# Stick-breaking attention: the cumulative sum as two float32r parts, the scores over 64 rows a head, and the gates of the two mixers summed by products with ones

## The chip, the cores and the metric

One core of a Trainium2 chip runs the whole program in one launch. The metric is device microseconds of that core; the time before the change is the median of three runs.

## What is computed

Two residual layers over 256 tokens of width 1024, float32 throughout. Layer 0 mixes tokens by stick-breaking attention, layer 1 by retention; each is followed by a mixture of 16 experts. A vector `c` modulates every sub-layer by shift, scale and gate (`adaLN`), and every sub-layer ends in a layer norm.

```python
def adaln_params(c, w, b):
    m = jax.nn.silu(c) @ w + b
    shift, scale, gate = jnp.split(m, 3, axis=-1)
...
# stick_breaking_attention, 16 heads of 64, one block of 128 queries
z = jnp.einsum('bhqd,bhkd->bhqk', qb, k) * scale
causal = key_pos[None, :] < q_pos[:, None]
log_keep = jnp.where(causal, jax.nn.log_sigmoid(-z), 0.0)
suffix = lax.cumsum(log_keep, axis=3, reverse=True) - log_keep
a = jnp.where(causal, jnp.exp(jax.nn.log_sigmoid(z) + suffix), 0.0)
o = jnp.einsum('bhqk,bhkd->bhqd', a, v)
...
x = layer_norm(DEEPNORM_ALPHA * x + (1.0 + gate) * y, ln_g[i, 0], ln_b[i, 0])
```

The gate of a mixer is thus a row of 1024 numbers, `1 + silu(c) @ w + b`, that multiplies the output of the mixer's last projection on every token.

## The kernel before

**Stages.** The program passes through attention (`STICK`), the first mixture (`SPARSE`), retention (`RETEN`) and the second mixture. Weights stream from memory through a ring of 1 MB buffers; SP issues all their transfers in one queue, and a transfer waits there until its buffer is free. A scheduler sets the order of the instructions on every engine when the program is built: it takes the order in which the code emits them as priority and its own estimate of durations, so each engine's queue is fixed when the program runs.

**Dense products.** `dense_feat` (L431) and `dense_tok` (L405) multiply by weights in two float32r parts. `pieces` (L384) loads 512 rows of weights and splits them in two pieces of 128x1024 numbers: ACT copies the piece to float32r (L381), DVE subtracts the copy from it (L382). Both parts lie in one buffer of the tag `w2`, which in the attention stage means one of the two `wp` buffers. `mm3` (L400) then makes three products a block (L401 to L403).

**Modulation.** `ada_part(i, j)` (L266) computes 512 columns of `silu(c) @ w` of sub-layer `i`; `j` 0 and 1 are the shift, 2 and 3 the scale, 4 and 5 the gate. Either TensorE makes the products (L277), or DVE does, by eight passes over 128x512 (L280, L282), which leave partial sums in every partition. Four products with two columns of ones (L292, `rest`) sum over the partitions and turn the result into columns, and DVE adds the bias (L293, L296). `plan` lists such parts and `fill` emits the next one between two dense products; the `rest` of a part is emitted at the following `fill`. Before a mixer's last projection `gate_row` (L351) turns the gate's columns into a row that stands in all partitions: eight products (L235) and two ACT copies (L357). Sub-layers 0 and 2 are the two mixers, 1 and 3 the mixtures.

**Attention.** It goes in two halves of eight heads. `stick_in` (L572) makes queries, keys and values of a half. Queries go to `qz`, where each head's 64 rows stand alone in 128 rows of zeros (L575, L579, L580), so that a product over 128 rows gives one head's scores. `stick_attn` (L590) takes two heads at a time, four times a half:

```python
a = z + causal                              # L600, DVE
e = ln(1 + exp(-|a|))                       # L602 to L604, ACT
e = max(a, 0) + e                           # L605, DVE: -log_keep
sx = negtri @ e, mones @ e[later keys]      # L608, L609, TensorE, float32
a = exp(a + sx)                             # L610 DVE, L611 ACT
o = v @ a                                   # L615, L616, TensorE
oh, ol = split_to(o)                        # L381 ACT, L382 DVE
```

Here L597 and L598 make the scores `z`. After the two halves `out_proj` (L558) multiplies by `sb_w_out` column half by column half; L564 multiplies by the gate, L565 adds to the residual. The router (`logits`) and the first mixture follow.

**Places in memory.** `HIGH` gives every name a place in the numbered slots. The two halves' `qz` fill slots 2 and 3; the mixture's first weights want slots 2, 4, 0 and 1 (`RINGS["moe1"]`).

## Time and profile before

| what | value |
|---|---|
| median of 3 runs | 924.22 us (921.85 to 925.86) |
| the profiled execution, its time / its span | 924.58 us / 922.9 us |
| TensorE busy | 852.6 us, 92% of the span |
| DVE busy | 500.6 us, 54% |
| ACT busy | 275.7 us, 30% |
| memory read | 307.12 MB, 334 GB/s over the span |

The span is what the profiler saw between first and last instruction; the execution took 1.7 us more. A busy share is a mean over stages with different limits, so it has to be read stage by stage. A matmul in a row of matmuls begins long before the one ahead of it has ended: the time that one costs is read from start to start, not from its duration. DVE's instructions overlap by some 0.09 us in the same way.

### The profile page before, as it was taken

The page shows a single profiled execution, that of the slowest core. Times are in us where ns is not written, and L with a number is a line of the kernel's source. Part 1 is how long each engine was busy: PE and PEld are TensorE (multiplying, and loading weights), DVE is VectorE, ACT ScalarE, POOL GpSimd, SP SyncE. Part 2 cuts the span into 40 slices and gives each one's busy share as a digit, 9 for nine tenths or more (in the row PEclk, how much of TensorE's full clock was granted, in tenths as well). Part 3 has the DMA queues.
Part 4 walks back from the last instruction along what each step waited for, and adds up shares of the span by engine and source line. Part 5 has one row for each costly group of instructions (what it writes and reads, how often), then busy time and mean ns, then how long its engine had stood idle before and what let it go on. Part 6 is the DMA issues. An engine that isn't in the chain of part 4 may idle for free. (4 is left out here: it accounts for less than half of the span.)

```text
span 922.9 us, 11147 instructions
## 1 busy us (share of the span) xinstructions
PE 852.6 (92%) x4339; PEld 522.0 (57%) x4339; DVE 500.6 (54%) x927; ACT 275.7 (30%) x386; POOL 25.5 (3%) x46
## 2 busy tenths in 40 slices
PE   5899999989969999999799999999979989999994
PEld 2598887765324434334578888888843444343331
DVE  1478889835341326321797898948655322333126
ACT  1446756252110101000544455646351101011010
POOL 1000000000000000000000020011000000000000
PEclk9999999979999999999899999999979999999998
DMA  8999998796999999999669778939739999999951
GB/s 304 384 387 387 335 330 310 288 368 228 420 413 386 417 420 414 417 406 357 224 227 363 275 274 273 320 101 361 299 134 390 415 416 418 415 415 418 416 221 45
DMA packets 93075, 309.01 MB, mean 335 GB/s; under 512 B 5876, under 2 KB 6316, under 8 KB 77140
## 3 DMA queue, kind: packets, MB, share of 16 engines
q1 hardware_dynamic: 93012, 308.19, 86.9%
q8 instruction: 37, 0.61, 0.3%
q14 instruction: 26, 0.21, 0.1%
HBM read 307.12 MB, written 1.05 MB: 334 GB/s over the span
## 5 line engine op out<-in xcount | busy, mean ns | idle before, releaser
L964 PE MATMUL ps<-s,xg 128*64 128x512 f32 x632 | 164.8, 595 | 1.4 <-DVEq L842 1.4
L964 PE MATMUL ps<-w,xg 128*64 128x512 f32 x392 | 113.2, 606 | 6.5 <-PEq L842 6.5
L964 PEld LDWEIGHTS ps<-s,xg 128*64 128x64 f32 x632 | 50.7, 137 | 85.7 <-issue 81.8
L382 DVE TENSOR_TENSOR wp<-w,wp 128x1024 fp32r<-128x1024 f32 x57 | 69.5, 1222 | 20.3 <-ACT wp L381 19.1
L381 ACT ACTIVATE wp<-w 128x1024 fp32r<-128x1024 f32 x57 | 59.8, 1056 | 66.2 <-PE ps L403 55.6
L1044 PE MATMUL ps<-w,hidT 128*64 128x512 f32 x248 | 71.4, 596 | 7.2 <-DVE hidT L1007 6.6
L997 DVE TENSOR_TENSOR mosg<-mosg,ps 128x512 f32<-128x512 f32 x16 | 11.0, 688 | 122.0 <-PE ps L964 122.0
L381 ACT ACTIVATE moyh<-moy 128x512 fp32r<-128x512 f32 x32 | 20.1, 629 | 174.0 <-DVE moy L1017 174.0
L489 DVE TENSOR_TENSOR res<-res,ps 128x512 f32<-128x512 f32 x64 | 41.0, 684 | 57.0 <-PE ps L1029 57.0
L964 PEld LDWEIGHTS ps<-w,xg 128*64 128x64 f32 x392 | 34.8, 139 | 64.6 <-issue 62.7
L282 DVE SCALAR_TENSOR_TENSOR s<-w,cact,s 128x512 f32<-128x512 f32 x88 | 65.9, 749 | 0.7
L1017 DVE SCALAR_TENSOR_TENSOR moy<-ps,cs,gate 128x512 f32<-128x512 f32 x32 | 24.0, 749 | 69.7 <-PE ps L1044 61.0
L1044 PE MATMUL ps<-s,hidT 128*64 128x512 f32 x200 | 60.5, 594 | 1.1 <-DVE hidT L1007 1.1
L402 PE MATMUL ps<-wp,hh 128*128 128x512 f32 (+1 forms) x144 | 56.5, 395 | 0.0
L403 PE MATMUL ps<-wp,hl 128*128 128x512 f32 x144 | 55.6, 391 | 0.0
L401 PE MATMUL ps<-wp,hh 128*128 128x512 f32 (+1 forms) x144 | 53.9, 395 | 0.0
L452 ACT ACTIVATE xg<-ps,mod 128x256 f32<-128x256 f32 x32 | 18.0, 564 | 109.4 <-PE ps L918 109.4
L993 ACT ACTIVATE mosg<-ps 128x512 f32<-128x512 f32 x16 | 9.6, 598 | 115.9 <-PE ps L964 115.9
L1044 PEld LDWEIGHTS ps<-w,hidT 128*64 128x64 f32 x248 | 22.1, 136 | 36.6 <-issue 27.1
L401 PE MATMUL ps<-s,wp 128*128 128x256 f32 x128 | 37.7, 297 | 0.6 <-DVE fcol L222 0.6
L402 PE MATMUL ps<-s,wp 128*128 128x256 f32 x128 | 37.3, 294 | 0.0
L403 PE MATMUL ps<-s,wp 128*128 128x256 f32 x128 | 36.1, 294 | 1.0 <-DVE wp L382 1.0
(342 smaller groups left out, 1550.7 us busy)
## 6 DMA issues: line engine op xcount, KB each, us to landing
s<-in_moe_w_up SPq DMA_DIRECT2D x41, 1024.0 KB, 12.3
w<-in_ada_w SPq DMA_DIRECT2D x39, 1024.0 KB, 6.6
s<-in_moe_w_gate SPq DMA_DIRECT2D x34, 1024.0 KB, 11.3
w<-in_moe_w_down SPq DMA_DIRECT2D x34, 1024.0 KB, 12.5
w<-in_moe_w_gate SPq DMA_DIRECT2D x30, 1024.0 KB, 14.0
s<-in_moe_w_down SPq DMA_DIRECT2D x26, 1024.0 KB, 16.1
w<-in_moe_w_up SPq DMA_DIRECT2D x19, 1024.0 KB, 16.7
w<-in_ret_w_in SPq DMA_DIRECT2D x18, 1024.0 KB, 7.1
```

The source lines that it names most:

```text
L282: V.scalar_tensor_tensor(e, wt[:, kk, :], cact[:, k:k + 1], e, op0=OP.mult, op1=OP.add)
L381: A.activation(hi, src, AF.Copy)
L382: return V.tensor_tensor(lo, src, hi, op=OP.subtract).ins
L401: T.matmul(dst, lh, rh, start=start, stop=False)
L402: T.matmul(dst, lh, rl, start=False, stop=False)
L403: state["mm"] = T.matmul(dst, ll, rh, start=False, stop=stop).ins
L452: return A.activation(dst, src, AF.Identity, scale=sc[:, k:k + 1], bias=sh[:, k:k + 1]).ins
L489: V.tensor_tensor(res[:, b, js], res[:, b, js], add, op=OP.add)
L964: state["mm"] = T.matmul(o[64 * u:64 * u + 64, :], xg[:, k, at:at + CAP], ts[u][kk], start=(k == 0), stop=(k == NK - 1)).ins
L997: V.tensor_tensor(sgt, sgt, pu, op=OP.mult)
L1017: front = V.scalar_tensor_tensor(y, py, cs, gate[:, js], op0=OP.mult, op1=OP.mult).ins
L1044: state["mm"] = T.matmul(py[64 * u:64 * u + 64, :], hidT[:, f, u * CAP:(u + 1) * CAP], ts[u][:, i, js], start=(f == 0), stop=(f == 3)).ins
```

## The change

Scores: queries are stored as they come, two heads in the upper and lower 64 rows of one tile (`qT`), with one copy for two heads where there were two, and without the memset. Each score product takes 64 rows of keys and of queries; the products of the two heads stand next to each other in the queue.

Cumulative sums: `e` is split into two float32r parts (`split_to`: an ACT copy and a DVE subtraction of 128x768) in a new tile `er` in slot 3, which also holds `negtri` and `mones` converted to float32r once a half. Each sum is then made twice, once for each part, in float32r.

Gates of the two mixers (sub-layers 0 and 2): a gate part's bias row is loaded into all partitions by a broadcast transfer, 1 is added, the partial sums are split into two float32r parts in a `w2` buffer, and two products with a full tile of ones give the row in every partition; one DVE instruction adds it to the bias. `gate_row` is no longer called for these two; for the mixtures it is unchanged.

```diff
-HIGH = {"STICK": {"hA": (0, 1), "qz": ((2, 0), (3, 0)), "k4": ((4, 0), (4, 1024), (5, 0), (5, 1024)),
-                  "sb": ((6, 0), (6, 768), (7, 0), (7, 768), (8, 640)), "aux": ((8, 0),),
+HIGH = {"STICK": {"hA": (0, 1), "qT": ((2, 0), (2, 1024)), "k4": ((4, 0), (4, 1024), (5, 0), (5, 1024)),
+                  "sb": ((6, 0), (6, 768), (7, 0), (7, 768), (8, 640)), "er": (3,), "aux": ((8, 0),),
...
+        V.tensor_copy(ones_r, ones)
...
+        elif j >= 4:
+            return ada_gate(i, j - 4, o if on_pe else e, 1.0 / 32.0 if on_pe else 1.0)
...
+    def ada_gate(i, j, e, scale):
+        if i not in gate_of:
+            gate_of[i] = tmp([P, D], "gate", 1)
+        gate = gate_of[i][:, 512 * j:512 * j + 512]
+        SY.dma_start(gate, ada_b[i // 2, i % 2].rearrange("(o d) -> o d", o=1)[:, 2 * D + 512 * j:2 * D + 512 * j + 512].to_broadcast([P, 512]))
+        V.tensor_scalar(gate, gate, 1.0, None, op0=OP.add)
+        parts = big([P, 2, 2, 512], "w2", F32R)
+        hi, lo = parts[:, 0, 0, :], parts[:, 0, 1, :]
+        split_to(hi, lo, e)
+        def rest():
+            t = ps(tag="po") if state["name"] == "RETEN" else ps()
+            T.matmul(t, ones_r, hi, start=True, stop=False)
+            T.matmul(t, ones_r, lo, start=False, stop=True)
+            V.scalar_tensor_tensor(gate, t, scale, gate, op0=OP.mult, op1=OP.add)
+        return rest
...
-        qz = big([P, 8, S], "qz")
-        G.memset(qz, 0.0)
+        qT = big([P, 4, S], "qT")
...
-            A.activation(qz[0:64, 2 * m, :], t[0:64, :], AF.Copy, scale=0.125)
-            A.activation(qz[64:128, 2 * m + 1, :], t[64:128, :], AF.Copy, scale=0.125)
+            A.activation(qT[:, m, :], t, AF.Copy, scale=0.125)
...
+        er = big([P, 2048], "er", F32R)
+        V.tensor_copy(er[:, 1536:1792], aux[:, 0:2 * P])
+        negtri, mones, causal = er[:, 1536:1664], er[:, 1664:1792], aux[:, 2 * P:5 * P]
...
-            for q in range(2):
-                T.matmul(z[:, q, 0:256], kT[:, m, 0:P], qz[:, 2 * m + q, :], start=True, stop=False)
-                T.matmul(z[:, q, 256:384], kT[:, m, P:S], qz[:, 2 * m + q, P:S], start=False, stop=True)
+            heads = [slice(0, 64), slice(64, 128)]
+            for q, hs in enumerate(heads):
+                T.matmul(z[:, q, 0:256], kT[hs, m, 0:P], qT[hs, m, :], start=True, stop=False)
+            for q, hs in enumerate(heads):
+                T.matmul(z[:, q, 256:384], kT[hs, m, P:S], qT[hs, m, P:S], start=False, stop=True)
...
+            eh, el = [er[:, 768 * u:768 * u + 768].rearrange("p (q n) -> p q n", q=2) for u in range(2)]
+            split_to(eh, el, e)
...
-            for q in range(2):
-                T.matmul(sx[:, q, 0:384], negtri, e[:, q, :], start=True, stop=False)
-                T.matmul(sx[:, q, P:2 * P], mones, e[:, q, 256:384], start=False, stop=True)
+            for part in (eh, el):
+                for q in range(2):
+                    T.matmul(sx[:, q, 0:384], negtri, part[:, q, :], start=(part is eh), stop=False)
+                for q in range(2):
+                    T.matmul(sx[:, q, P:2 * P], mones, part[:, q, 256:384], start=False, stop=(part is el))
...
-        gate = gate_row(2)
+        gate = gate_of[2]
...
-    gate = gate_row(0)
+    gate = gate_of[0]
```

`ones_r` is filled in `vectors`, the branch with `ada_gate` stands in `ada_part` behind the one for odd `i`, `gate_row(2)` stood in `retention` and `gate_row(0)` behind the two halves of attention. In the changed program the lines from L210 on have other numbers: `split_to` is L405 (ACT) and L406 (DVE) there, DVE's passes of `ada_part` L284 and L286, the attention's DVE lines L626, L631 and L640, and `out_proj`'s multiplication by the gate L588.

**What moves, first place: ACT between the first queries and the first keys.** Before, ACT splits the last piece of query weights (`wp_341`) and at once the first piece of key weights (`wp_392`), then copies the queries out:

```order
L381 ACTIVATE wp_314<-lo_312 128x1024
L381 ACTIVATE wp_341<-lo_312 128x1024
L381 ACTIVATE wp_392<-w_390 128x1024
L579 ACTIVATE s_251<-ps_254 64x256
L580 ACTIVATE s_251<-ps_254 64x256
...
L381 ACTIVATE wp_419<-w_390 128x1024
L381 ACTIVATE wp_448<-w_446 128x1024
```

In the changed program the same stretch reads:

```order
L405 ACTIVATE wp_315<-lo_313 128x1024
L405 ACTIVATE wp_342<-lo_313 128x1024
L405 ACTIVATE wp_388<-s_82 128x512
L602 ACTIVATE s_253<-ps_255 128x256 x2
L602 ACTIVATE s_253<-ps_256 128x256 x2
L405 ACTIVATE wp_395<-w_393 128x1024
L405 ACTIVATE wp_422<-w_393 128x1024
```

The gate's partial sums (`wp_388`) have taken the turn of one of the two `wp` buffers, and the first piece of key weights (`wp_395`) now stands behind the copies of the queries.

**Second place: DVE from the seventh addition of the cumulative sums to the eighth and last.** Before:

```order
L610 TENSOR_TENSOR s_82<-s_82,px_1138 128x768
L605 SCALAR_TENSOR_TENSOR s_207<-s_207 128x768
L282 SCALAR_TENSOR_TENSOR s_82<-w_1209,cact,s_82 128x512
L382 TENSOR_TENSOR wp_1344<-w_1342,wp_1344 128x1024
L280 TENSOR_SCALAR s_82<-w_1313,cact 128x512
L610 TENSOR_TENSOR s_207<-s_207,px_1162 128x768
```

In the changed program (the dots stand for seven passes L286, one L284, and one row each of L299 and L302):

```order
L631 SCALAR_TENSOR_TENSOR s_209<-s_209 128x768
L286 SCALAR_TENSOR_TENSOR s_82<-w_1237,cact,s_82 128x512
L640 TENSOR_TENSOR s_82<-s_82,px_1176 128x768
L406 TENSOR_TENSOR s_1102<-s_209,s_1102 128x768
L284 TENSOR_SCALAR s_82<-w_1251,cact 128x512
...
L406 TENSOR_TENSOR ol_252<-po_1187,oh_251 128x256
L286 SCALAR_TENSOR_TENSOR s_82<-w_1348,cact,s_82 128x512
L640 TENSOR_TENSOR s_209<-s_209,px_1206 128x768
```

The subtraction that makes the second part of `e` (L406 of 128x768) stands between, and ten instructions of `ada_part` (two L284, eight L286) where two stood.

## Rows read from the trace of the kernel before

**Rows 1.** Busy time of each engine in stretches of the span: queries and keys of the first half of attention; from the first scores on to the second half; the second half up to the first multiplication by the gate; the rest of the projection; the router; the first mixture; retention. Columns: stretch, its length, busy us of PE, PEld, DVE, ACT and POOL with the number of instructions, granted TensorE clock, share of the DMA engines, GB/s.
```profile
core 0: us, PE busy (x) PEld busy (x) DVE busy (x) ACT busy (x) POOL busy (x), PEclk, DMA share, GB/s
41.30:73.80 32.50, 30.88 (x219) 29.90 (x220) 26.34 (x39) 14.85 (x21) 0.00 (x0) 1.00 1.05 387
73.80:127.10 53.30, 53.30 (x360) 46.49 (x359) 47.74 (x68) 36.09 (x46) 0.00 (x0) 1.00 0.98 358
127.10:170.00 42.90, 42.72 (x236) 33.75 (x235) 39.63 (x66) 28.61 (x35) 0.00 (x0) 1.00 0.83 295
170.00:181.20 11.20, 10.87 (x72) 9.77 (x70) 10.13 (x23) 0.00 (x0) 0.55 (x1) 1.00 0.76 284
200.00:220.00 20.00, 16.43 (x85) 11.73 (x86) 10.75 (x36) 9.40 (x14) 0.00 (x0) 0.80 0.44 165
220.00:440.00 220.00, 204.91 (x961) 82.86 (x958) 75.94 (x157) 21.80 (x39) 0.00 (x0) 0.98 1.01 404
460.00:650.00 190.00, 190.00 (x926) 157.88 (x926) 156.39 (x259) 96.70 (x132) 17.61 (x32) 1.00 0.78 277
```

**Rows 2.** Who waited for whom in the attention stage (40 to 182 us), TensorE first, then DVE: us in total, times, the longest.
```profile
PE ps L403 <- DVE wp L382: 1.0, 2, 0.5
DVE wp L382 <- ACT wp L381: 10.0, 10, 2.5
DVE s L605 <- ACT s L604: 2.9, 2, 2.3
```

**Rows 3.** TensorE in order of time from 82 to 105 us: start, duration, line, operation, tiles, shape, number of records (a float32 product has two). The cumulative sums of one pair of heads and the product behind them; the scores of one pair between two products with 512 and 256 columns; the passage to a product with values; the products with values of two heads side by side.
```profile
82.39 0.81 PE L608 MATMUL px<-s 128*128 128x384 f32 x2
...
84.04 0.48 PE L402 MATMUL ps<-wp,s 128*128 128x512 f32 x1
...
86.21 0.39 PE L403 MATMUL ps<-wp,s 128*128 128x512 f32 x1
86.44 0.59 PE L597 MATMUL pz<-s,s 128*128 128x256 f32 x2
...
87.67 0.36 PE L401 MATMUL ps<-s,wp 128*128 128x256 f32 x1
...
88.10 0.28 PE L401 MATMUL ps<-s,wp 128*128 128x256 f32 x1
88.22 0.28 PE L402 MATMUL ps<-s,wp 128*128 128x256 f32 x1
...
89.53 0.28 PE L401 MATMUL ps<-s,wp 128*128 128x256 f32 x1
89.74 0.65 PE L615 MATMUL po<-s,s 128*64 128x256 f32 x2
...
103.88 0.66 PE L615 MATMUL po<-s,s 128*64 128x256 f32 x4
104.36 0.40 PE L616 MATMUL po<-s,s 128*64 128x128 f32 x4
```

**Rows 4.** TensorE, the gate of the attention: four sums over partitions and the product behind them, and the two pieces of the row.
```profile
74.65 0.95 PE L292 MATMUL ps<-con,s 128*128 128x2 f32 x8
75.46 0.48 PE L402 MATMUL ps<-wp,s 128*128 128x512 f32 x1
...
146.81 0.94 PE L235 MATMUL ps<-con,sums 128*128 128x128 f32 x6
148.48 1.38 PE L235 MATMUL ps<-con,sums 128*128 128x128 f32 x10
```

**Rows 5.** DVE in order of time: the first addition of the attention; four neighbours, for their distances from start to start; the last cumulative addition, the first and the last multiplication by the gate.
```profile
73.83 0.95 DVE L600 TENSOR_TENSOR s<-pz,s 128x768 f32<-128x768 f32 x1
...
84.08 0.74 DVE L282 SCALAR_TENSOR_TENSOR s<-lo,cact,s 128x512 f32<-128x512 f32 x1
84.73 1.22 DVE L382 TENSOR_TENSOR wp<-lo,wp 128x1024 fp32r<-128x1024 f32 x1
85.87 0.95 DVE L610 TENSOR_TENSOR s<-s,px 128x768 f32<-128x768 f32 x1
86.73 0.48 DVE L280 TENSOR_SCALAR s<-w,cact 128x512 f32<-128x512 f32 x1
...
163.49 0.95 DVE L610 TENSOR_TENSOR s<-s,px 128x768 f32<-128x768 f32 x1
...
170.03 1.29 DVE L564 TENSOR_TENSOR s<-ps,gate 128x512 f32<-128x512 f32 x2
...
180.75 0.42 DVE L564 TENSOR_TENSOR s<-po,gate 128x256 f32<-128x256 f32 x1 [0.62 <-PE po L403]
```

**Rows 6.** ACT in order of time: the split of the first piece of key weights, the first copy of queries, the splits of the next two pieces; a load of a function table in the first pair of heads. Last, TensorE at its first product with the second piece of key weights.
```profile
54.11 1.06 ACT L381 ACTIVATE wp<-w 128x1024 fp32r<-128x1024 f32 x1 [2.56 <-PE ps L403]
56.33 0.38 ACT L579 ACTIVATE s<-ps 64x256 f32<-64x256 f32 x1 [1.16 <-PE ps L403]
...
59.48 2.01 ACT L381 ACTIVATE wp<-w 128x1024 fp32r<-128x1024 f32 x2
...
76.20 1.28 ACT L603 ACT_TABLE_LOAD   x1
...
60.59 0.39 PE L401 MATMUL ps<-s,wp 128*128 128x256 f32 x1
```

**Rows 7.** DVE at the end of the first mixture: the last reading of its gate.
```profile
442.45 0.75 DVE L1017 SCALAR_TENSOR_TENSOR moy<-ps,cs,gate 128x512 f32<-128x512 f32 x1 [0.25 <-PE ps L1059]
```

More of the change, by code (lines that the diff above doesn't have):

```diff
@@ L240, in tile_trunk @@
     trig = keep([P, 3, NB, 64], "trig")
+    ones_r = keep([P, P], "ones_r", F32R)
+    gate_of = {}
     def rotary_tables():
@@ L587, in stick_in, with stick_attn @@
         fill()
-        return qz, kT, v
-    def stick_attn(oh, ol, aux, qz, kT, v, half):
-        negtri, mones, causal = aux[:, 0:P], aux[:, P:2 * P], aux[:, 2 * P:5 * P]
+        return qT, kT, v
+    def stick_attn(oh, ol, aux, qT, kT, v, half):
+        er = big([P, 2048], "er", F32R)
+        V.tensor_copy(er[:, 1536:1792], aux[:, 0:2 * P])
+        negtri, mones, causal = er[:, 1536:1664], er[:, 1664:1792], aux[:, 2 * P:5 * P]
         if half == 0:
```

## Prediction, before the run

> **What bounds the kernel now.** I read the busy time by stretch first [rows 1]. In the attention stage TensorE is busy for 53.3 of 53.3 us and 42.7 of 42.9 us, with no pause that the profile shows; in retention for 190 of 190. In the first mixture it is the transfers: 404 GB/s at a share of 1.01 for 220 us. Ahead of the mixture, at the router, the transfers rest (share 0.44, so some 11 of 20 us are free). So the mixture starts from full buffers, and what the attention stage gains or loses arrives at the end one for one as long as it is under some 11 us.
>
> The second column to read is DVE's. From the first addition of the attention (73.8 us) to the end of the projection (181.2 us) are 107.4 us, and DVE works 47.7 + 39.6 + 10.1 = 97.5 us of them [rows 1]. TensorE sets the pace, but DVE has a reserve of 9.9 us only. Who waits for whom agrees [rows 2]: TensorE waits 1.0 us for DVE's weight splits; DVE waits 10.0 us for ACT's, which in turn wait for TensorE to free a buffer, and 2.9 us for ACT's logarithm.
>
> **The change on TensorE.** Durations overlap, so I take distances from start to start. The scores of a pair of heads take 86.44 to 87.67, 1.23 us [rows 3]; two heads side by side should halve that: 8 x 0.61 = 4.9 us. No row shows two row halves at work at once. The nearest is the product with values, whose two heads stand in two column halves: the two products of 256 columns take 103.88 to 104.36, 0.48 us [rows 3], where two thirds of one head's 0.61 us, 0.41, would be one such product alone. So I take the half, and keep no saving as the other end.
>
> The cumulative sums take 82.39 to 84.04, 1.65 us [rows 3]. In float32r 256 columns take 0.12 us (88.10 to 88.22) and 512 take 0.23 (86.21 to 86.44), hence 384 about 0.175 and 128 between 0.06 and 0.12. Two parts of two heads: 4 x 0.175 + 4 x 0.06 to 0.12 = 0.94 to 1.18 us, a saving of 0.5 to 0.7 us a pair, 8 x 0.6 = 4.8 us.
>
> A gate loses two groups of four sums over partitions, 0.81 us each (74.65 to 75.46), and its row, 0.94 + 1.38 less 0.3 us of run-out = 2.0 us [rows 4], and gains four products of 512 columns, 0.92 us: -2.7 us for each mixer. TensorE thus loses 4.9 + 4.8 + 2.7 = 12.4 us of work in the attention stage and 2.7 us in retention.
>
> The passage between kinds of product is not free. 89.53 to 89.74 is 0.21 us where a product of that size takes 0.12 [rows 3]: 0.09 us at a passage from the full array to column halves. Sixteen new passages to row halves and back at that price are 1.4 us of TensorE. [...]
>
> **The change on DVE.** Here work is added, and the order shows where. Between the first addition and the last multiplication by the gate the changed queue has eight subtractions of 128x768, one conversion of the constants (128x256), one multiplication of the gate (128x512) and one more weight split (it stood ahead of the first addition before); two small ones are gone. Start to start, an addition of 128x768 takes 0.86 us (85.87 to 86.73), a weight split 1.14 (84.73 to 85.87), a pass of 128x512 0.65 (84.08 to 84.73) [rows 5]; the conversion is a third of the addition's size, 0.3. Sum: 8 x 0.86 + 0.3 + 0.65 + 1.14 - 0.2 = 8.8 us. DVE's 97.5 us become 106.3 us in a stretch that lasts 107.4 us today. **DVE takes TensorE's place**, and the 12.4 us have nowhere to go: even with no pause at all the stretch would be 1.1 us shorter.
>
> How much pause stays? Today 9.9 us, most of it behind ACT's splits [rows 2], which a faster TensorE releases earlier. What stays is the start: the first pair's logarithm stands behind two table loads of 1.28 us each, of which one is shown [rows 6], 2.3 us of DVE's pause today [rows 2], and the changed queue of ACT has five such loads in place of three. In the last pairs, where I follow the three queues row by row, DVE hardly waits: its queue puts ten instructions of `ada_part` between the seventh and the eighth cumulative addition, where two stood, so the eighth is late because DVE is full. Bounds: 0 and the present 9.9 us; I take 4, the two waits for the logarithm and about a microsecond more. The stretch: 106.3 + 4 = 110.3, **+2.9 us** (-1.1 to +8.8).
>
> The tail is inside that sum. Today 6.5 us lie between the last cumulative addition and the first multiplication by the gate (163.49 to 170.03) [rows 5]; in the changed queue DVE alone has 10.5 us of work between them (the addition itself, five weight splits, five passes, the last subtraction of the output). The last addition itself comes some two microseconds earlier if pauses are 4 us.
>
> **Ahead of the first scores.** A gate part borrows one of two `wp` buffers. Today the first piece of key weights is split at 54.11, ahead of the query copies at 56.33, and TensorE gets the second piece at 60.59 [rows 6]. In the changed order the first piece stands behind the copies. These are four of about 0.39 us in place of eight: they end near 57.9, the split 1.06 us later, so TensorE begins the keys at 59.0, needs 24 x 0.12 = 2.9 us for the piece, and gets to the second near 61.9: +1.3 us. The gate's own products run in that pause, and four sums over partitions (0.81 us) that lay behind it are gone. Before the first values the same loan is covered by the copies of the keys and the first scores. I take **+0.8 us** (-0.8 to +2).
>
> **Retention.** TensorE is the bound (190 of 190) while DVE has 156 of 190 us [rows 1]; DVE's added 3 us (two additions to the bias, two subtractions, two multiplications) fit. The 2.7 us arrive, less half a microsecond for the borrowed buffer: **-2.2 us** (-2.7 to 0). The gate's two transfers wait until the first mixture has read its gate for the last time, at 442.45 [rows 7]; weights of retention stand behind them on SP, but they are the weights of the values, wanted only after queries and keys. **At nothing** I put: the earlier pair of such transfers (0.5 MB, 1.4 us at the 387 GB/s of that stretch [rows 1]; TensorE waits for no transfer there [rows 2]), the memset, ACT's 6 us for eight copies (ACT has 36 of 53 and 29 of 43 us), and the mixture's first weights for slot 2, issued later because both halves now use that slot: covered by the free 11 us at the router, and their price beyond that is what is left over.
>
> **Sum**: 2.9 + 0.8 - 2.2 = +1.5 us on the profiled execution's 924.6, which is 0.4 us above the median of the runs: 926.1 us. A measurement of this kernel tells about 0.5%, 4.6 us, from no change.
>
> **Rivals.**
> *A, TensorE stays the bound* and its savings arrive: pauses of DVE vanish or its passes of `ada_part`, which the mixture wants only later, slip behind the projection. With all of it 924.6 - 12.4 - 2.7 = 909.5; with half of the attention's share 924.6 - 6.2 - 2.7 = 915.7. For it speaks that TensorE never waits today; against it the sum on DVE and the fixed order, which keeps 46 such passes ahead of the first multiplication by the gate as against 45. I give it 0.17, at about 915.
> *B, the chain of a pair becomes the bound*: split, second product, addition and exponential of a pair follow one another with a single `er`, `pz` and `px`, 0.75 us of ACT and 0.86 of DVE longer, and TensorE has less other work to put between. Its place is the second half, from 127 us on; its price is DVE's pause staying at the present 9.9 us: 110.3 becomes 116.2, so 924.6 + 8.8 + 0.8 - 2.2 = 932. It decides once DVE's pauses there exceed 6 us. For it: two engines at 99% of a stretch seldom meet without pauses. I give it 0.27.
> *C, the row halves don't run side by side*: 4.9 us stay on TensorE. It then has about 107 - 4.8 - 2.7 + 1.4 = 101 us of work in the stretch, still under DVE's 106.3; I add a microsecond, 927. I give it 0.10. [...]
>
> **The numbers.** Forecast 0.46 (its own range 921 to 931), A 0.17, C 0.10, B 0.27. Faster by over 0.5% is A but for its edge and a trace of the forecast: 0.17. Slower by over 0.5% is most of B and the upper fifth of the forecast: 0.33. Within it: 0.50. The range 917 to 934 leaves out the deeper half of A and the top of B.
>
> **What would show it.** DVE busy for over 104 us from the first addition of the attention to the end of the projection, a stretch of 108 to 113 us, and TensorE waiting there for DVE for several microseconds where it waited 1; the eighth cumulative addition no more than 8 us before the first multiplication by the gate would speak against my tail. Score products of a pair at 0.6 us and sums at 0.9 to 1.2 us confirm the TensorE part; retention shorter by about 2 us the last. I am wrong if the stretch falls below 105 us, or if DVE is under 95% busy in it while the time rises.

## The result, and the profile after

The changed kernel takes 931.46 us (median of 12 runs, 928.08 to 933.21), the kernel before 925.36 beside it (12 runs, 921.85 to 927.84): a ratio of 1.0062, with a 95% interval of 1.0045 to 1.0079. It is slower, by 6 us where I forecast 1.5. The profiled execution took 933.2 us with a span of 931.5, against 924.6 and 922.9 before; it was the longest of the 12, so the two profiles differ by more (8.6 us) than the medians (6.1). One run of the kernel called h2 below took 1701.9 us and is left out of its figures.

First the busy time by stretch, which answers [rows 1]. Columns as there; the first rows are the stages of the attention, then four slices of its second half, then retention.

```profile
41.50:74.00 32.50, 29.44 (x206) 27.67 (x206) 27.07 (x41) 13.29 (x19) 0.00 (x0) 0.95 1.05 386
74.00:127.35 53.35, 51.59 (x358) 45.99 (x359) 48.69 (x66) 40.68 (x49) 0.00 (x0) 0.97 0.89 315
127.35:177.75 50.40, 43.26 (x215) 34.94 (x215) 48.52 (x78) 30.20 (x37) 0.00 (x0) 0.80 0.84 302
177.75:189.00 11.25, 11.25 (x77) 10.34 (x76) 9.49 (x23) 0.57 (x1) 0.56 (x1) 1.00 0.78 301
...
140.00:146.00 6.00, 4.72 (x32) 3.98 (x32) 6.00 (x10) 2.64 (x3) 0.00 (x0) 0.81 1.04 405
146.00:152.00 6.00, 3.39 (x18) 2.10 (x14) 6.00 (x15) 4.36 (x7) 0.00 (x0) 0.50 1.01 415
152.00:158.00 6.00, 2.75 (x9) 2.38 (x9) 6.00 (x10) 4.71 (x8) 0.00 (x0) 0.50 0.80 271
158.00:164.00 6.00, 6.00 (x18) 5.08 (x19) 5.49 (x11) 0.59 (x1) 0.00 (x0) 0.50 0.66 218
...
462.00:655.00 193.00, 192.31 (x923) 159.23 (x922) 162.18 (x263) 98.99 (x135) 15.15 (x32) 1.00 0.79 282
```

From the first addition to the end of the projection DVE now works 48.7 + 48.5 + 9.5 = 106.7 us of 115.0. In the first half of the heads TensorE is still the busier of the two (51.6 of 53.4 us, DVE 48.7). In the second half DVE is busy for 48.5 of 50.4 us, while TensorE, which had no pause there before, has work for 43.3. In the slices from 140 to 158 us DVE is at 6.00 of 6.00 and TensorE falls to 2.75. TensorE did not only wait: from 146 to 164 its granted clock is 0.50, where the kernel before had 1.00 in its whole second half [rows 1]. Up to 158 us DVE is full, so the clock sets nothing there; from 158 to 164, where TensorE is at 6.00 and DVE at 5.49, it may. In retention it is busy for 192.3 of 193.0 us as before, and DVE for 162.2.

The next rows are TensorE's timeline in that place (start, duration, engine, line, tile, count), and answer [rows 3].

```profile
140.14 0.51 PE L637 MATMUL px<-s 128*128 128x384 f32 x2
140.49 0.33 PE L639 MATMUL px<-s 128*128 128x128 f32 x2
140.66 1.00 PE L298 MATMUL ps<-con,s 128*128 128x2 f32 x8
...
143.79 0.98 PE L637 MATMUL px<-s 128*128 128x384 f32 x2 [1.28 <-DVE s L640]
144.57 0.52 PE L639 MATMUL px<-s 128*128 128x128 f32 x2
...
150.28 1.13 PE L645 MATMUL po<-s,s 128*64 128x256 f32 x4 [2.45 <-ACT s L641]
...
157.91 1.87 PE L298 MATMUL ps<-con,s 128*128 128x2 f32 x8 [2.48 <-ACT s L289]
...
160.64 0.63 PE L427 MATMUL ps<-wp,ol 128*128 128x512 f32 x1
161.06 0.63 PE L425 MATMUL ps<-wp,oh 128*128 128x512 f32 x1
...
166.68 0.39 PE L425 MATMUL ps<-wp,oh 128*128 128x512 f32 x1
166.91 0.39 PE L426 MATMUL ps<-wp,oh 128*128 128x512 f32 x1
```

One float32r part of a pair's sums takes 140.14 to 140.66, 0.52 us, so two take 1.04 where one float32 pass, as the kernel before made it, took 1.65 [rows 3]. The waits in brackets end with DVE, or with an ACT instruction that itself follows DVE's. At the granted clock of 0.50 a product of 512 columns takes 0.42 us (160.64 to 161.06); from 166 to 168 us, at 1.00, it takes 0.23 (166.68 to 166.91).

DVE's timeline at the tail answers the last rows of [rows 5]:

```profile
160.67 3.90 DVE L286 SCALAR_TENSOR_TENSOR s<-w,cact,s 128x512 f32<-128x512 f32 x5
165.87 0.48 DVE L284 TENSOR_SCALAR s<-w,cact 128x512 f32<-128x512 f32 x1 [1.29 <-ACT s L289]
...
167.26 0.95 DVE L640 TENSOR_TENSOR s<-s,px 128x768 f32<-128x768 f32 x1
...
177.09 0.74 DVE L286 SCALAR_TENSOR_TENSOR s<-w,cact,s 128x512 f32<-128x512 f32 x1
177.75 0.68 DVE L588 TENSOR_TENSOR s<-ps,gate 128x512 f32<-128x512 f32 x1
```

The eighth cumulative addition starts at 167.26 and the first multiplication by the gate at 177.75, with no wait in front: 10.5 us of DVE's own queue, in which it has no pause. (TensorE has none there either.)

ACT's timeline ahead of the first scores answers [rows 6]:

```profile
53.61 0.63 ACT L405 ACTIVATE wp<-s 128x512 fp32r<-128x512 f32 x1 [3.52 <-DVE s L286]
54.82 1.37 ACT L602 ACTIVATE s<-ps 128x256 f32<-128x256 f32 x4 [0.58 <-PE ps L427]
56.08 1.06 ACT L405 ACTIVATE wp<-w 128x1024 fp32r<-128x1024 f32 x1
58.43 1.06 ACT L405 ACTIVATE wp<-w 128x1024 fp32r<-128x1024 f32 x1 [1.29 <-PE ps L319]
```

The copy of the gate part waits 3.5 us in ACT's queue for DVE's passes, and the copies of the queries and the first key weights (56.08, where they stood at 54.11) come after it. The second piece of key weights waits until the gate's products (L319) give the borrowed buffer back.

Where the 8.6 us of the two profiles arise, from the starts of the same instructions in both:

| from ... to | before | after | longer by |
|---|---|---|---|
| start ... first addition of the attention | 73.8 | 74.0 | 0.2 |
| ... last multiplication by its gate | 106.9 | 114.5 | 7.6 |
| ... first weighted output of the first mixture | 56.9 | 58.5 | 1.5 |
| ... last one | 204.8 | 199.5 | -5.3 |
| ... first rotation of retention | 22.5 | 23.7 | 1.2 |
| ... last multiplication by its gate | 199.1 | 195.9 | -3.3 |
| ... first weighted output of the second mixture | 44.6 | 45.5 | 1.0 |
| ... last one | 199.2 | 205.2 | 6.0 |
| ... end | 15.1 | 14.8 | -0.3 |

The two mixtures, which the change does not touch, have moved against each other. Each has one jump over code that is not run (`spill`, L872 now, L842 before). These are TensorE's two jumps in the changed kernel (shortest, median, longest ns, first and last start), and the wait behind the second:

```profile
L872 PEldq COMPARE_BRANCH  x2: 445/3298/6150, 278.6 to 742.9; - x2
```

```profile
PE ps L994 <- PEq L872: 6.3, 1, 6.3
```

Of the two jumps one takes 0.4 us and one 6.2. Before, it was the same (0.41 and 6.2), but there TensorE waited 6.5 us in the first mixture, now in the second. That trades 5.3 against 6.0 us and hardly touches the sum.

### The profile page after: what moved, and what is told of

Same layout as the page of the kernel before. It is cut to its first block, busy times and chain, and to the rows that moved or that the text cites. A ratio compares the mean times of both kernels' runs of the same rounds, so it can differ in the third digit from the quotient of the medians.

```text
span 931.5 us, 11029 instructions
## 1 busy us (share of the span) xinstructions
PE 849.0 (91%) x4283; PEld 517.6 (56%) x4283; DVE 512.7 (55%) x942; ACT 281.3 (30%) x387; POOL 19.5 (2%) x44
## 5 line engine op out<-in xcount | busy, mean ns | idle before, releaser
L994 PE MATMUL ps<-s,xg 128*64 128x512 f32 x632 | 169.1, 610 | 6.3 <-PEq L872 6.3
L406 DVE TENSOR_TENSOR wp<-w,wp 128x1024 fp32r<-128x1024 f32 x55 | 67.0, 1219 | 16.4 <-ACT wp L405 15.5
L405 ACT ACTIVATE wp<-w 128x1024 fp32r<-128x1024 f32 x55 | 58.0, 1057 | 56.6 <-PE ps L427 48.9
L405 ACT ACTIVATE moyh<-moy 128x512 fp32r<-128x512 f32 x32 | 20.1, 629 | 174.0 <-DVE moy L1047 174.0
L286 DVE SCALAR_TENSOR_TENSOR s<-w,cact,s 128x512 f32<-128x512 f32 x88 | 65.2, 745 | 0.7
L426 PE MATMUL ps<-wp,hh 128*128 128x512 f32 (+1 forms) x148 | 58.3, 395 | 0.0
L427 PE MATMUL ps<-wp,hl 128*128 128x512 f32 (+1 forms) x148 | 57.1, 392 | 0.0
L425 PE MATMUL ps<-wp,hh 128*128 128x512 f32 (+1 forms) x148 | 54.6, 396 | 0.7 <-ACT wp L405 0.7
## 6 DMA issues: line engine op xcount, KB each, us to landing
s<-in_moe_w_up SPq DMA_DIRECT2D x41, 1024.0 KB, 14.8
s<-in_moe_w_gate SPq DMA_DIRECT2D x34, 1024.0 KB, 15.1
```

What stands on the lines that cost most here:

```text
L286: V.scalar_tensor_tensor(e, wt[:, kk, :], cact[:, k:k + 1], e, op0=OP.mult, op1=OP.add)
L405: A.activation(hi, src, AF.Copy)
L406: return V.tensor_tensor(lo, src, hi, op=OP.subtract).ins
L425: T.matmul(dst, lh, rh, start=start, stop=False)
L426: T.matmul(dst, lh, rl, start=False, stop=False)
L427: state["mm"] = T.matmul(dst, ll, rh, start=False, stop=stop).ins
```

## Experiments

The theories. **D**: DVE's work bounds the attention stage, as forecast. **B**: the chain of a pair does (the rival of that name). **C**: row halves don't run side by side. **W**: the gate parts' loan of a weight buffer, and the place of their split in ACT's queue, delay the weights; I had priced this at 0.8 us ahead of the first scores.

All were timed against the kernel before, in four sessions in which its median was 924.7 to 925.5 us; the ratio is to the one beside. *Stretch* is from the first addition of the attention to 0.7 us behind the start of the last multiplication by its gate, *DVE* the busy time in it, *last* the start of that last multiplication (all from the profile, us); *rest* is the span from there on.

| kernel | first addition | stretch | DVE | last | rest | median | ratio (95%) |
|---|---|---|---|---|---|---|---|
| before | 73.8 | 107.6 | 97.7 | 180.8 | 742.2 | 925.4 | 1 |
| changed | 74.0 | 115.2 | 106.9 | 188.5 | 743.0 | 931.5 | 1.0062 (1.0045 to 1.0079) |
| p1 scores only | 72.4 | 107.2 | 98.0 | 178.9 | 745.1 | 924.7 | 0.9993 (0.9974 to 1.0013) |
| p2 scores, sums | 71.5 | 113.6 | 104.5 | 184.4 | 745.1 | 930.5 | 1.0051 (1.0032 to 1.0070) |
| p3 gates only | 77.6 | 110.8 | 98.7 | 187.7 | 743.4 | 931.8 | 1.0069 (1.0050 to 1.0087) |
| p4 scores, gates | 72.2 | 111.6 | 100.0 | 183.1 | 740.1 | 926.9 | 1.0017 (1.0005 to 1.0030) |
| g1 late split | 70.7 | 117.1 | 108.5 | 187.1 | 741.4 | 928.8 | 1.0044 (1.0022 to 1.0066) |
| g2 p4, own buffer | 70.0 | 110.0 | 100.5 | 179.3 | 740.0 | 920.0 | 0.9949 (0.9928 to 0.9969) |
| g3 GpSimd subtracts | 74.2 | 117.2 | 110.3 | 190.6 | 738.8 | 931.5 | 1.0074 (1.0048 to 1.0101) |
| g4 modulation on TensorE | 71.6 | 110.1 | 92.7 | 181.0 | 739.1 | 926.0 | 1.0012 (0.9993 to 1.0030) |
| h1 g2, one part on TensorE | 70.6 | 107.0 | 95.1 | 176.9 | 746.4 | 927.0 | 1.0019 (1.0006 to 1.0032) |
| h2 own buffer | 71.0 | 112.8 | 105.6 | 183.1 | 743.8 | 928.5 | 1.0044 (1.0029 to 1.0059) |
| h3 h2 and g4 | 70.9 | 106.4 | 92.3 | 176.6 | 740.2 | 920.4 | 0.9963 (0.9944 to 0.9982) |
| h4 copy twice | 73.4 | 114.7 | 106.4 | 187.4 | 746.7 | 934.3 | 1.0096 (1.0072 to 1.0120) |

*Last* carries the verdicts on the attention stage. *Rest* varies from 738.8 to 746.7 among kernels whose edits leave it alone but for retention's 3.3 us, so a time by itself tells no more than about 3 us of an edit. A profile, too, is one execution, no kernel was profiled twice, and the executions of one kernel spread over 2 to 8 us. The profiles of g3, g4, h1 and h3 are of their fastest execution, those of the changed kernel and h4 of their slowest. A difference in *last* that the medians don't bear out is therefore to be read with care.

### The parts one by one: p1, p2, p3, p4

p1 and p3 add one part of the change to the kernel before; p2 and p4 are the changed kernel with one part taken back. The hunks are those of the diff above: p1 has the ones on `qT` and `T.matmul(z`, p3 those on `ada_gate`, `gate_of` and `ones_r`. p2 leaves out those of p3, p4 those on `er`:

```diff
-            eh, el = [er[:, 768 * u:768 * u + 768]... for u in range(2)]
-            split_to(eh, el, e)
             sx = ps([P, 2, 512], "px")
-            for part in (eh, el):
-                ...
+            for q in range(2):
+                T.matmul(sx[:, q, 0:384], negtri, e[:, q, :], start=True, stop=False)
+                T.matmul(sx[:, q, P:2 * P], mones, e[:, q, 256:384], start=False, stop=True)
```

Expected of p1: 

> The kernel before with one part of the change alone: the scores over 64 rows a head. Theory D (DVE is what bounds the changed kernel's attention stage): here DVE gets no new work (97.5 us in the stretch from the first addition to the end of the projection), TensorE loses up to 4.9 us of 107, so the stretch shrinks by 2 to 5 us and the time to 920.5 to 923.5, ratio 0.995 to 0.998. Theory C (row halves don't run side by side, or the passages eat the gain): scores of a pair stay near 1.2 us, ratio 0.999 to 1.002. Theory B (the chain of a pair bounds): no gain either although the products of a pair take 0.6 us.

Expected of p2: 

> The changed kernel without its gate part: scores over 64 rows and sums in two float32r parts, gates as before. Theory D: DVE 97.5 + 7.2 = 104.7 us in the stretch, pauses 5 to 8, so the stretch is 110 to 113 us and the time 928 to 931, ratio 1.003 to 1.006; retention as before. If instead the gates' loan of a weight buffer is what costs (theory W), this kernel is at 918 to 924, ratio below 0.999.

Expected of p3: 

> The kernel before with the gate part alone. Theory D: DVE 97.5 + 1.6 = 99.1 us, TensorE loses 2.7 us in the stretch and 2.7 in retention: time 919 to 922, ratio 0.993 to 0.997; retention shorter by 2 to 3.5 us as in the changed kernel. Theory W (the loan of a weight buffer delays the splits): the attention stage longer by 2 to 5 us, time 924 to 927, ratio 1.000 to 1.003.

Expected of p4: 

> The changed kernel with its cumulative sums back in one float32 part: scores over 64 rows and gates by products with ones. Theory D: DVE 99.1 us in the stretch, TensorE 107 - 4.9 - 2.7 = 99.7: both near 100 with pauses of 3 to 6, so the stretch is 102 to 105 us, the time 915 to 920, ratio 0.990 to 0.995, clearly below both kernels. Theories B and W: at or above the time before, ratio 1.000 to 1.005.

p1, TensorE's timeline, one pair's scores:

```profile
84.56 0.70 PE L596 MATMUL pz<-s,s 64*128 64x256 f32 x4
85.10 0.39 PE L598 MATMUL pz<-s,s 64*128 64x128 f32 x4
85.42 0.39 PE L401 MATMUL ps<-s,wp 128*128 128x256 f32 x1
```

A pair takes 84.56 to 85.42, 0.86 us in place of 1.23 [rows 3]: more than the half that I took, less than C's. (What the 0.25 us above the half are, no run shows.) Eight times 0.37 are 3 us; 1.9 of them reach the last multiplication, and the time does not show it. D's 2 to 5 us in the stretch were missed: it shrank by 0.4, with DVE at 98.0 us of 107.2, and where the rest went stays open. The time is what B and C had said of it.

p3 is the surprise. It adds 1 us to DVE in the stretch and, by my sum, takes 2.7 off TensorE, and yet the last multiplication comes 6.9 us later, 3.8 of them already at the first addition, and the time is 931.8. TensorE's waits before the first addition, in p3:

```profile
PE ps L425 <- ACT wp L405: 3.6, 1, 3.6
PE ps L425 <- DVE fcol L223: 0.6, 1, 0.6
PE ps L427 <- DVE wp L406: 0.5, 1, 0.5
```

The 3.6 us are the split that stands behind the gate part in ACT's queue. W holds, and larger than I had written down for it. p4 missed D's numbers too: a stretch of 111.6 us where D had 102 to 105, and 926.9 us, in the range of B and W. It has the loan as well, but that is not the whole reason: g2 below, which is p4 without the loan, still has a stretch of 110.0. There DVE works 100.5 us and pauses 9.5, where D allowed 3 to 6, and TensorE is busy for 106.6; why stays open. p2, without the loan, came out near D's numbers, 930.5: DVE 104.5 us of 113.6, with pauses of 9.1 where D had 5 to 8. Read as differences at the last multiplication: the float32r sums cost 5.6 us on top of the scores (p2 less p1) and 5.4 on top of scores and gates (changed less p4); the gates cost 4.1 to 6.9.

### What the loan costs: g1, g2, h2

g1 emits the split of a gate part one filling later, in `rest`, when its sum is complete. g2 is p4 with the gate parts in slot 3 (tag `gp`), which is free there. h2 is the whole change with a buffer of its own for the parts of the attention's gate: 768 numbers a partition under the tag `gp`, and the last 256 of `er`, which is now taken once for both halves. (The hunks show the lines that matter.)

```diff
 g1
-        parts = big([P, 2, 2, 512], "w2", F32R)
-        hi, lo = parts[:, 0, 0, :], parts[:, 0, 1, :]
-        split_to(hi, lo, e)
         def rest():
+            parts = big([P, 2, 2, 512], "w2", F32R)
+            hi, lo = parts[:, 0, 0, :], parts[:, 0, 1, :]
+            split_to(hi, lo, e)
 g2
+        if state["name"] == "STICK":
+            if j == 0:
+                gate_of["parts"] = big([P, 2, 2, 512], "gp", F32R)
+            parts = gate_of["parts"][:, j:j + 1]
 h2
+            hi = gate_of["parts"][:, 0:512]
+            los = [gate_of["parts"][:, 512:768], gate_of["er"][:, 1792:2048]]
```

Expected of g1: 

> The changed kernel, but a gate part is split (ACT's copy, DVE's subtraction) one filling later, together with its products, when its sum is complete. Theory W (the early split stands in ACT's queue and waits 3.5 us for DVE's passes, with the query copies and the next key weights behind it, and holds a weight buffer meanwhile): TensorE gets the first key weights some 3 us earlier, the last multiplication by the attention's gate moves from 188.5 to 184 to 186 us, the time to 927 to 929, ratio 1.002 to 1.004. Theory D (DVE is full from the first addition on, whatever comes ahead): under 1.5 us of it arrive, ratio 1.005 to 1.007.

Expected of g2: 

> The changed kernel with its cumulative sums back in one float32 part, and with the attention's gate parts in the buffer that the two parts of the sums had, instead of a borrowed weight buffer. Theory W, loan: against the same kernel with the borrowed buffer (926.9 us, last multiplication at 183.1) some 2 to 4 us come back, last multiplication at 179 to 181, time 923 to 925, ratio 0.997 to 0.999. If the loan costs nothing, 926 to 928, ratio 1.001 to 1.003.

Expected of h2: 

> The whole change, but the attention's gate parts in a buffer of their own instead of a borrowed weight buffer (the second part of a gate in two pieces of 256 columns). Theory W, loan: the same 3.8 us as in the kernel without float32r sums arrive, last multiplication by the attention's gate at 184 to 186 instead of 188.5, time 926 to 928.5, ratio 1.001 to 1.004. Theory D (DVE is full from the first addition on, so an earlier start is waited away): at 186 or later, 928.5 to 931, ratio 1.004 to 1.007.

g1 shows D and W at once. The first addition comes 3.4 us earlier (70.65), as W said, but the last multiplication only 1.4 (187.1), as D said: the stretch is 2.0 us longer, and DVE has 1.6 us more to do in it. Its ratio, 1.0044, lies between the two.

g2 gains 3.8 us on p4 at the last multiplication, as W said, and 6.9 in time, more than W said; it is faster than the kernel before. h2 gains 5.4 on the changed kernel at the last multiplication, more than either theory had; of its time, 928.5, less arrives, and the intervals of the two ratios overlap. These are h2's halves and then its ACT queue:

```profile
71.00:119.29 48.29, 48.29 (x351) 43.42 (x349) 46.68 (x64) 38.12 (x46) 0.00 (x0) 1.00 0.97 352
119.29:171.19 51.90, 45.16 (x218) 35.65 (x217) 46.54 (x74) 30.99 (x39) 0.00 (x0) 0.77 0.80 296
```

```profile
52.58 1.06 ACT L413 ACTIVATE wp<-w 128x1024 fp32r<-128x1024 f32 x1 [2.57 <-PE ps L435]
53.54 0.61 ACT L319 ACTIVATE gp<-s 128x512 fp32r<-128x512 f32 x1
54.74 1.38 ACT L610 ACTIVATE s<-ps 128x256 f32<-128x256 f32 x4 [0.58 <-PE ps L435]
```

The key weights are split at 52.58 again, ahead of the gate part. The first half takes 48.3 us in place of 53.4, with 1.6 us of DVE's pause in place of 4.7; but in the second half 5.4 us of pause appear where the changed kernel had 1.9, with TensorE at a granted clock of 0.77. So the loan is worth 5.4 us at the last multiplication, 3.0 of them ahead of the first addition, and it explains where most of the first half's pauses came from, but not all pauses go with it: 7.2 us stay.

### Less work for DVE: g3, g4, h3, h1

g3 moves the subtraction of the sums to GpSimd. g4 lets TensorE make three modulation parts of the first mixture; h3 does that in h2; h1 does it for one part in g2.

```diff
 g3
-            split_to(eh, el, e)
+            A.activation(eh, e, AF.Copy)
+            G.tensor_tensor(el, e, eh, op=OP.subtract)
 g4, h3
-    plan(1, range(6))
+    plan(1, range(3))
+    plan(1, range(3, 6), on_pe=True)
 h1
+    plan(1, range(3))
+    plan(1, range(3, 4), on_pe=True)
+    plan(1, range(4, 6))
```

Expected of g3: 

> The changed kernel with the subtraction that makes the second part of the sums' operand moved from DVE to GpSimd, which is idle there. No row shows such a subtraction on GpSimd; between 0.9 us (DVE's) and 3 us. Theory D (DVE's work bounds): DVE loses 8 x 0.86 = 7 us of 107, the last multiplication by the attention's gate comes at 183 to 186 instead of 188.5, time 926 to 929, ratio 1.000 to 1.004. Theory B (the chain of a pair bounds): the chain gets longer by 0 to 2 us a pair, the time stays or rises, ratio 1.006 to 1.015.

Expected of g4: 

> The changed kernel with three of the six modulation parts of the first mixture made by TensorE instead of DVE: 24 passes of 128x512 less on DVE, 24 x 0.65 = 15.6 us, for some 24 products of 512 columns in four column groups on TensorE (an estimate of 2 to 3 us a part). Theory D: DVE falls to some 91 us in the stretch, TensorE at about 105 bounds it; last multiplication by the attention's gate at 182 to 185 instead of 188.5, time 925 to 928, ratio 0.999 to 1.003. Theories B and W: what holds the stretch is not DVE's sum, so at most 1.5 us arrive, ratio 1.005 to 1.008.

Expected of h3: 

> The kernel before this one with three modulation parts of the first mixture made by TensorE as well. Theories D and W together (DVE's work bounds the changed kernel's stretch, and the loan delays its start): DVE near 92 us, the loan gone: against 926.0 us with the loan, 922 to 924.5, ratio 0.996 to 0.999. If the loan was only paid for where DVE was full: as with the loan, 1.000 to 1.002.

Expected of h1: 

> The kernel with scores over 64 rows, gates by products with ones in a buffer of their own and sums in one float32 part (919.95 us), now with one of the six modulation parts of the first mixture made by TensorE instead of DVE. There DVE had 100.5 us of work in a stretch of 110 and TensorE 106.6: if DVE's work still bounds, its 5.2 us less bring 1 to 4 us, 916 to 919, ratio 0.991 to 0.994; if TensorE bounds, its 2.5 us more cost 1 to 3, 921 to 923, ratio 0.996 to 0.998.

g4, its whole stretch:

```profile
71.61:181.67 110.06, 107.43 (x704) 86.65 (x708) 92.69 (x142) 70.41 (x86) 0.55 (x1) 1.00 0.91 330
```

DVE has 14.2 us less to do. The last multiplication comes 7.5 us earlier (181.0 for 188.5), 5.1 of them in the stretch; the time falls by 5.4 to 926.0. TensorE is busy for 107.4 of 110.1 us at a granted clock of 1.00: with DVE relieved the bound has gone back to TensorE. That is what D said (182 to 185 and 925 to 928), and B and W allowed 1.5 us. Two things blur the size: the granted clock rises with the relief, from 0.90 to 1.00 over the stretch, and the profile is of g4's fastest execution (the two profiles differ by 11.4 us in all). The intervals of the two ratios don't overlap. h3 has both remedies and gains 11.9 us on the changed kernel at the last multiplication (h2's 5.4 and g4's 7.5 together are 12.9) and 11.1 in time. Against g4 the buffer of its own brings 5.7 us in time, more than expected, so the loan costs something where DVE is not full, too.

g3 decides nothing between D and B, for a reason that its timelines show, GpSimd's first and DVE's next:

```profile
83.74 2.51 POOL L634 TENSOR_TENSOR s<-s,s 128x768 fp32r<-128x768 f32 x1 [82.76 <-ACT s L633]
92.20 1.84 POOL L634 TENSOR_TENSOR s<-s,s 128x768 fp32r<-128x768 f32 x1 [5.95 <-ACT s L633]
```

```profile
82.66 0.74 DVE L286 SCALAR_TENSOR_TENSOR s<-lo,cact,s 128x512 f32<-128x512 f32 x1
83.32 1.22 DVE L406 TENSOR_TENSOR wp<-w,wp 128x1024 fp32r<-128x1024 f32 x1
84.46 2.35 DVE L286 SCALAR_TENSOR_TENSOR s<-lo,cact,s 128x512 f32<-128x512 f32 x1
...
92.25 0.94 DVE L641 TENSOR_TENSOR s<-s,px 128x768 f32<-128x768 f32 x1
```

A pass that takes 0.74 us takes 2.35 when it meets a subtraction on GpSimd (83.74 to 86.25), and ends half a microsecond after it. DVE lost eight subtractions of 0.86 us and is yet busy for 3.4 us more.

h1 moved the attention as D said, last multiplication 2.4 us earlier than in g2, and yet took 7 us longer. The loss lies in the first mixture, where the edit adds no work. TensorE's waits there, in h1, and its timeline:

```profile
PE ps L993 <- issue: 6.3, 1, 6.3
```

```profile
262.83 0.73 PE L1058 MATMUL ps<-moyl,pt 128*128 128x512 f32 x2 [0.42 <-DVE moyl L411]
269.88 12.55 PE L993 MATMUL ps<-w,xg 128*64 128x512 f32 x48 [6.31 <-issue]
```

At the first mixture's jump TensorE stands for 6.3 us with no wait shown. In g2 it stands there for 1.5 us, and h1's *rest* is 6.4 us longer than g2's (746.4 and 740.0). So the time of h1 decides nothing between my two expectations.

### The chain of a pair: h4

```diff
+            A.activation(eh, e, AF.Copy)
             split_to(eh, el, e)
```

Expected: 

> The changed kernel with ACT's copy of the sums' operand to float32r made twice: 0.75 us of ACT more in the chain of each pair, and not a microsecond more of DVE. Theory B (the chain of a pair bounds): 4 to 6 us longer, last multiplication by the attention's gate at 192 to 194, time 935 to 938, ratio 1.010 to 1.014. Theory D (DVE's work bounds): at most 1.5 us, 931 to 933, ratio 1.005 to 1.008.

```profile
73.41:188.12 114.71, 104.65 (x656) 88.94 (x660) 106.42 (x166) 77.16 (x94) 0.55 (x1) 0.94 0.87 310
```

ACT has 5.7 us more in the stretch, one copy a pair, all in the chain. The stretch did not grow (114.7 for 115.2), and the last multiplication comes at 187.4, no later than 188.5. So by the profile B does not hold the attention stage. The granted clock is 0.94 there and 0.90 in the changed kernel, so that a small cost may be hidden. The time rose by 2.8 us all the same, between the two expectations; by the profile the part behind the attention, where the edit changes nothing, is 3.7 us longer. Why stays open, and the time alone would not rule B out.

## Why the prediction was right where it was, and wrong in size

**The bound: right, for the second half above all.** The sum on DVE was 106.3 us; it is 106.7. The tail was 10.5 us; it is 10.5. The stretch grew although TensorE's products became cheaper, and g4, which takes three modulation parts off DVE and gives them to TensorE, gets 7.5 us back at the last multiplication. Rival A is out. In the first half of the heads TensorE stayed the busier engine.

**The signs that I had named** did not all come. DVE's work is over 104 us, and TensorE waits for DVE, or for ACT behind it, where it hardly waited. But the stretch, 115.0 us, lies above the 108 to 113, the scores of a pair above the 0.6, and DVE is busy for 93% of the stretch (106.7 of 115.0) while the time rose: under 95% was a sign of being wrong. It is 91% in the first half, 96% in the second and 84% in the projection. The time, 931.5, lies above the forecast's own 921 to 931 and within the whole range only by the part that was there for B. That it lies within is luck for the forecast.

**The term that failed: DVE's pauses.** I took 4 us, "the two waits for the logarithm and about a microsecond more". They are 115.0 - 106.7 = 8.3 us: 4.7 in the first half, 1.9 in the second, 1.8 in the tail, near what they were before (9.9). I had read a row wrongly: I put most of the 9.9 us down to the waits for ACT's splits, 10.0 us in [rows 2]. But those rows begin at 40 us, and most of these waits lie ahead of the first addition. DVE's waits before, from 73.8 to 181.2 us, and then in the changed kernel, from 74 to 189.2:

```profile
DVE wp L382 <- ACT wp L381: 4.0, 6, 1.2
DVE s L605 <- ACT s L604: 2.9, 2, 2.3
```

```profile
DVE s L631 <- ACT s L630: 1.8, 2, 0.9
DVE wp L406 <- ACT wp L405: 1.5, 3, 1.0
DVE s L284 <- ACT s L289: 1.3, 1, 1.3
DVE s L588 <- PE ps L427: 1.1, 1, 1.1
```

The splits could thus give back 4.0 us at most, and gave 2.5; the logarithm gave 1.1. Waits that I had put at nothing took their place: 1.3 us for ACT's copy of a modulation part (0.5 before) and 1.7 for the projection's products (1.0 before). W has its share, too. By h2 the loan makes 3.1 us of the first half's pause; with it gone others arise in the second half, and the total falls to 7.2 only. What sets those 7 us stays open: by h4's profile it is not ACT's share of the chain, and it is not the loan alone. I should have kept a pause near the 9.9 us of before until a row of the same stretch spoke for less.

**Ahead of the first scores: right in number, wrong in kind.** I took +0.8 us; the first addition came 0.2 later. But h2 has it at 71.0: without the loan the change would have brought 2.8 us here, and the loan took 3.0. (p1, with the new scores alone and so with fewer query copies, brings 1.4; what the rest is, no run tells.) I had read the order of ACT's queue correctly, but had left out the 3.5 us that ACT waits in front of the gate part's split for DVE's passes. Nor had I seen that the loan delays the weights of the values, too: 12 of their products of 512 columns stand ahead of the first addition in h2, and 2 in the changed kernel.

**TensorE.** Scores: 3 us, not 4.9 (0.86 a pair, not 0.61). Sums: 1.04 us a pair without waits, in the 0.94 to 1.18 that I gave. Neither entered the sum, since I took DVE for the bound.

**Retention.** I took -2.2 (-2.7 to 0); it is -3.3, in p3 the same (from the first rotation to the last multiplication 195.8 us). It is 0.6 us more than the 2.7 that I counted for TensorE's products; where that comes from, no run tells.

**Rivals.** B named 932 us, and the time is 931.5; but it put the pause into the second half, where DVE is 96% busy and pauses 1.9 us, and h4's profile speaks against its mechanism. The number was met by another way. C is out: at 0.86 us a pair six tenths of the saving that I counted on were there.

**The sum.** By the profiles: attention +7.8 where I had +3.7, retention -3.3 where I had -2.2, all else +4.1 where I had nothing; 8.6 in place of 1.5. The runs have 6.1. The 4.1 are not explained by the change: p1 and p2 show +3.0 in the rest of the span with no edit there, and each profile is one execution.

## What to carry to other kernels

When two engines are both near full, add the work of the second before counting what the first one loses. The float32r sums, for which DVE pays 6.9 us (the changed kernel against p4), cost 5.4 to 5.6 us at the last multiplication. The parts that cost DVE little were the better change by themselves, once they borrowed no buffer (g2, 0.9949). With DVE relieved the whole change is faster than the kernel before, too (h3, 0.9963 with an interval of 0.9944 to 0.9982), but no faster than g2: no run here shows the float32r sums to be worth anything, and none has g2 with DVE relieved as far as in h3. Read a row of waits in the window that the sum is about. A borrowed buffer costs what waits in front of its release and what stands behind its filling in that engine's queue (5.4 us at the last multiplication here, by h2), so price the wait of the instruction that fills it (3.5 us here), too. And judge a small edit by the stage that it touches: the profiles here differ by some 3 us in stages that nobody edited, and it is open how much of that is the build and how much the single execution.

## What the runs showed of the hardware

- **One of TensorE's two jumps took 6 us.** Of the two jumps over `spill`, one took 5.9 to 6.2 us and the other 0.41 to 0.45 in each of the profiles of before, changed, p1 to p4, h3 and h4. The long one is the first in before, p1, p2 and h3 and the second in the others, though none of the edits touches either. What decides which of them is long, no run shows.
- **Beside a subtraction on GpSimd a pass on DVE took three times as long.** In g3 a pass of 0.74 us on DVE (82.66) took 2.35 (84.46) beside a subtraction on GpSimd. That one took 2.51 us where it began inside a split of DVE's (83.74), and another took 1.84 (92.20) beside an addition that reads one operand from `px` and kept its 0.94 us (92.25).
- **TensorE's granted clock fell behind a wait and rose after work without a pause.** In the changed kernel it is 1.00 from 140 to 143 us and 0.50 from 143.8 to 164, behind a wait of 1.3 us for DVE and with two waits of 2.5 us in it. Two products of 384 columns take 0.78 us there (143.79 to 144.57) where they took 0.35 (140.14 to 140.49), and a product of 512 columns takes 0.42 (160.64 to 161.06). From 166 to 168 us the clock is 1.00, after TensorE had worked without a pause from 158 on, and such a product takes 0.23 us (166.68 to 166.91).
